# The first two modulation rows of a conditioned encoder layer: weights as the stationary operand, three feature tiles ahead

## The chip, the cores and the metric

The kernel runs on one core of a Trainium2 chip. The metric is the device time of one execution in microseconds; lower is better. Five engines work side by side, each with its own queue of instructions: TensorE (PE in the profile; its weight loads are listed apart as PEld), VectorE (DVE), ScalarE (ACT), GpSimd (POOL) and SyncE (SP), which here only issues transfers.

## The reference, cut to what matters

One layer of a streaming encoder, for a prompt of 1024 tokens and a sample of 32 tokens that share all weights (1056 tokens in all, width 1024). Each of the two groups has its own conditioning vector c.

```
mod = silu(c) @ w_ada + b_ada            # (1024) @ (1024, 9*1024): nine rows of 1024 for each group
modulate(x, k) = x * (1 + mod[3k+1]) + mod[3k]
x = layer_norm(x, ln_in_g, ln_in_b)      # shared input norm
f = swiglu(modulate(x, 0), ffn1_w1, ffn1_w3, ffn1_w2)
x = layer_norm(ALPHA * x + 0.5 * (1 + mod[2]) * f, ...)
...                                      # mixer (RG-LRU and spatial gating), then a second FFN
```

Only rows 0 and 1 of mod (shift and scale of the first FFN) are touched here. They are needed first of all: nothing of the first FFN can be multiplied before them.

## The kernel before, in words

All activations are held transposed: features on the 128 partitions, tokens along the free axis, in three chunks of 384, 384 and 288 tokens. A feature tile f is 128 of the 1024 features; there are eight. Every large matmul works on float32 split into a high and a low part of the type float32r, as three products (high*high, high*low, low*high). The helper `mm` (L152, L153 in the profile) issues all of them; `h_mm` (L565) issues the three products of one weight tile, one feature tile and one chunk.

The kernel begins with `startup` (L376). Nine row tiles of x (eight of 128 tokens, one of 32) come in by SP. In a loop over i, DVE takes the statistics of tile i (`stats`, L418, L419, L562), GpSimd makes the inverse root (L563), ACT (L428) or for tiles 5 and 8 DVE (L425) normalises tile i-1 (`norm`), TensorE transposes it (`turn`, L438), and ACT (L450) or, from tile 6 on, DVE (L448) copies tile i-2 out of PSUM (`out`). The first feature tile's modulation product is issued at i = 9 (`ada_mm`), behind the last turn. Then two of the four half tiles of weights of the first FFN tile are split (`w_split`: high part on ACT at L210, low part at L211).

`ffn_first` (L575) follows. For each feature tile f: `ada_t` turns the product's row into a column by two small transposes and makes the coefficients A and B of that tile with b_ada and the input norm's gain and bias (L589 to L594); `mod_a` applies them on ACT (L539); the next tile's product is issued (`ada_mm(f + 1)`) and its row copied out (`ada_row`, L515); `mod_b` makes xh and xl, the high and low parts (L548 or L546, L549); the weights of a tile further on are split (`ada_load`); and TensorE does step f - 1 of the first FFN tile (`mms`): 18 matmuls into six PSUM banks, two weight matrices by three chunks by three products.

In the product for the modulation, c is the stationary operand and w_ada streams. For feature tiles 0 to 3 both are plain float32 (silu(c), 128x2, stationary; 256 columns of w_ada moving, rows 0 and 1 side by side). For tiles 4 to 7 both are split: c4 holds high and low parts of silu(c) in four columns, and w_ada comes as high and low part. The result lies along a row: group on the partition, feature along the free axis.

In `startup` and `ffn_first` the instructions of DVE, ACT and GpSimd keep the order in which the code issues them, and those of TensorE do so throughout. Behind `ffn_first`, a planner orders DVE, ACT and GpSimd by its own estimate of when things are ready. There, work beside the main stream is issued by generators (`go`, `poll`) at due times counted in TensorE work: the residual's scaling, the other seven rows of mod (`ada_rest`, DVE, L714), and `combs` (L810), which forms sums and differences of blocks of xh and xl on GpSimd and later DVE (L801 to L804) for the fast product of the later FFN tiles.

Buffers: ring "wh" (eight tiles) holds split weights and, before them, the float32 modulation weights of tiles 0 to 3; ring "raw" (five) holds weights as they come; the pool `gpool` is opened behind `startup` in the space of its x tiles. [...]

## Time and profile before

| | us |
|---|---|
| median of three runs | 1881.07 |
| lowest, highest | 1878.71, 1882.26 |
| the profiled execution's own time | 1877.9 |
| its span, first to last instruction | 1876.1 |
| first transposes start | 10.74 |
| first FFN matmul starts | 40.75 |
| granted TensorE clock, mean | 0.994 |

In the timeline rows, the columns are start, duration, engine, line, operation, output and inputs, shapes (stationary, then moving for a matmul), the number of merged instructions, and in brackets how long the engine had been idle and what ended that. In rows of groups, "busy, mean ns of one" stand behind the bar, then the idle time ahead of them. Rows of windows give, for a stretch of time, its length, each engine's busy time, then the granted clock, the share of the DMA engines and GB/s. A float32 product that isn't float32r has more than one record in the trace.

### The profile page before, as it was taken

How to read it: one execution, taken by the hardware profiler on the slowest of the kernel's cores; microseconds unless marked ns; L12 is line 12 of the kernel's file. 1: busy time of each engine (PE TensorE's matmuls, PEld its weight loads, DVE VectorE, ACT ScalarE, POOL GpSimd, SP SyncE). 2: the span in 40 equal slices, each digit the busy share in tenths (PEclk: the TensorE clock that was granted, in tenths of full speed). 3: DMA queues.
4: the chain of work that ended last, by engine and by line, in shares of the span. 5: the costliest groups of instructions: out<-in, count | busy, mean ns of one | idle time of the engine just before them, and what ended most of it. 6: DMA issues, size and time to landing. Idle time of an engine off the chain costs nothing.

```text
span 1876.1 us, 28307 instructions
## 1 busy us (share of the span) xinstructions
PE 1823.0 (97%) x11295; PEld 1784.8 (95%) x11295; DVE 1329.9 (71%) x2362; ACT 684.0 (36%) x1200; POOL 556.2 (30%) x416
## 2 busy tenths in 40 slices
PE   6999999999999999999999999999999999999997
PEld 3889999999999999989889999999999999999996
DVE  6889878978888866873986476965655564555676
ACT  5551332233233223355554447132232233223324
POOL 2493434243333424022000000134233333423410
PEclk9999999999999999999999999999999999999998
DMA  7352353444445433212012300120121112011102
GB/s 295 124 181 68 124 191 124 143 161 165 159 130 189 136 115 125 90 75 88 4 53 81 136 25 33 45 68 23 46 67 46 45 46 68 26 59 52 46 1 93
DMA packets 51028, 175.70 MB, mean 94 GB/s; under 512 B 7504, under 2 KB 10192, under 8 KB 50128
## 3 DMA queue, kind: packets, MB, share of 16 engines
q1 hardware_dynamic: 31984, 102.77, 16.4%
q10 hardware_dynamic: 18912, 71.11, 11.0%
q8 instruction: 89, 1.46, 0.3%
q14 instruction: 43, 0.35, 0.1%
HBM read 165.13 MB, written 8.74 MB: 93 GB/s over the span
## 4 chain that ended last, share of the span: by engine, by line
PE 81%; DVE 10%; ACT 3%; POOL 3%; issue 1%; DMA 1%; SPq 0%; ACTq 0%; DVEq 0%; POOLq 0%
PE ps L153 79%; DVE xl L549 1%; PE psl L153 1%; DVE wh L211 1%; POOL s L801 1%; ACT t L539 1%; DVE xa L960 1%; PE psa L153 1%; POOL tx L804 1%; DVE araw L714 1%; POOL s L802 1%; POOL tx L803 0%; ACT xh L546 0%; DVE s L801 0%; POOL raw L242 0%
## 5 line engine op out<-in xcount | busy, mean ns | idle before, releaser
L153 PE MATMUL ps<-xh,wh 128*128 128x384 f32 (+1 forms) x3824 | 900.8, 318 | 2.6 <-ACT xh L546 1.8
L153 PEld LDWEIGHTS ps<-xh,wh 128*128 128x128 f32 x3824 | 660.8, 188 | 6.2 <-ACT xh L546 2.2
L153 PE MATMUL ps<-xl,wh 128*128 128x384 f32 (+1 forms) x1912 | 607.7, 318 | 4.8 <-DVE xl L549 4.7
L210 ACT ACTIVATE wh<-raw 128x512 fp32r<-128x512 f32 x452 | 281.9, 629 | 596.2 <-PE ps L153 471.2
L153 PE MATMUL ps<-g,wh 128*128 128x384 f32 (+1 forms) x2808 | 459.4, 323 | 1.9 <-DVE s L675 0.8
L153 PEld LDWEIGHTS ps<-g,wh 128*128 128x128 f32 x2808 | 453.1, 188 | 3.6 <-DVE s L675 1.1
L211 DVE TENSOR_TENSOR wh<-raw,wh 128x512 fp32r<-128x512 f32 x283 | 214.0, 760 | 229.6 <-ACT wh L210 226.9
L153 PEld LDWEIGHTS ps<-xl,wh 128*128 128x128 f32 x1912 | 359.2, 188 | 9.0 <-DVE xl L549 7.9
L211 POOL TENSOR_TENSOR wh<-raw,wh 128x512 fp32r<-128x512 f32 x169 | 246.3, 1459 | 385.6 <-ACT wh L210 384.7
L960 DVE SCALAR_TENSOR_TENSOR xb<-ps,gt,xb 128x384 f32<-128x384 f32 (+1 forms) x352 | 151.4, 484 | 77.9 <-PE ps L153 64.7
L714 DVE SCALAR_TENSOR_TENSOR araw<-araw,cb 128x1024 f32<-128x1024 f32 x112 | 160.0, 1432 | 11.8 <-DMA araw<-ada 7.8
L153 PE MATMUL ps<-tx,wh 128*128 128x384 f32 x912 | 167.1, 338 | 0.0
L240 POOL TENSOR_TENSOR raw<-raw 128x512 f32<-128x512 f32 x38 | 54.5, 1433 | 365.8 <-DVE wh L211 348.5
L153 PEld LDWEIGHTS ps<-tx,wh 128*128 128x128 f32 x912 | 159.8, 188 | 0.0
L960 DVE SCALAR_TENSOR_TENSOR xa<-ps,gt,xa 128x384 f32<-128x384 f32 (+1 forms) x320 | 135.2, 480 | 7.2 <-PE ps L153 7.0
L210 ACT ACTIVATE g<-s 128x384 fp32r<-128x384 f32 (+1 forms) x126 | 61.4, 494 | 164.4 <-DVE s L675 164.4
L852 DVE TENSOR_TENSOR s<-s,ps 128x384 f32<-128x384 f32 x152 | 83.8, 552 | 45.0 <-PE ps L153 43.2
L211 DVE TENSOR_TENSOR g<-s,g 128x384 fp32r<-128x384 f32 (+1 forms) x126 | 93.5, 748 | 21.6 <-ACT g L210 20.5
L563 POOL TENSOR_TENSOR r<-r,half 128x3 f32<-128x3 f32 x8 | 7.1, 886 | 305.7 <-DVE r L562 305.7
L153 PE MATMUL ps<-T,wh 128*128 128x384 f32 x456 | 85.6, 335 | 0.0
L242 POOL TENSOR_TENSOR raw<-raw 128x512 f32<-128x512 f32 x38 | 57.5, 1513 | 85.9 <-DVE wh L211 83.6
L153 PEld LDWEIGHTS ps<-T,wh 128*128 128x128 f32 x456 | 80.2, 188 | 0.0
(246 smaller groups left out, 1649.3 us busy)
## 6 DMA issues: line engine op xcount, KB each, us to landing
raw<-wst SPq DMA_DIRECT2D x156, 512.0 KB, 3.7
araw<-ada ACTq DMA_DIRECT2D x112, 512.0 KB, 3.4
wnat<-ada SPq DMA_DIRECT2D x8, 512.0 KB, 10.2
raw<-ada SPq DMA_DIRECT2D x8, 512.0 KB, 4.0
xt<-x SPq DMA_DIRECT2D x7, 512.0 KB, 8.0
araw<-wst ACTq DMA_DIRECT2D x6, 512.0 KB, 4.1
sp<-xa ACTq DMA_DIRECT2D x2, 1536.0 KB, 5.3
xb<-sp ACTq DMA_DIRECT2D x2, 1536.0 KB, 9.3
```

Of the source, the lines that this page charges most:

```text
L153: self.nc.tensor.matmul(out, a, b, start=start, stop=stop, skip_group_check=True)
L210: self.nc.scalar.activation(dst_h, src, AF.Copy)
L211: (e or self.nc.vector).tensor_tensor(dst_l, src, dst_h.bitcast(F32), ALU.subtract)
L240: G.tensor_tensor(a["A21"], a["A11"], a["A21"], ALU.subtract)
L242: G.tensor_tensor(a["A22"], a["A22"], a["A21"], ALU.subtract)
L539: self.nc.scalar.activation(tmp[:, j, a:a + w], X[:, k, a:a + w], AF.Identity, scale=self.A[:, s, k, v:v + 1], bias=self.B[:, s, k, v:v + 1])
L549: V.tensor_tensor(xl, tmp, xh.bitcast(F32), ALU.subtract)
L714: V.scalar_tensor_tensor(raws[n], raws[n], 1.0, cb, ALU.mult, ALU.mult, accum_out=self.mod[:, m, f, v:v + 1])
L801: e.tensor_tensor(r, x[i][:, k, :].bitcast(F32), y[i][:, k, :].bitcast(F32), op)
L802: e.tensor_tensor(t, t, u, ALU.add)
L852: self.mark = V.tensor_tensor(out, x, ps[:, :n], ALU.add)
L960: self.mark = V.scalar_tensor_tensor(X[:, m, a + o:a + o + w], ps[:, o:o + w], self.gt[:, s, m, v:v + 1], X[:, m, a + o:a + o + w], ALU.mu ...
```

## The change

The product is turned round. The weights of w_ada become the stationary operand, 128x128 in plain float32, and silu(c) moves, two columns (one for each group). The result comes out as a column, features on partitions, two numbers each, for rows 0 and 1 in four columns of one PSUM bank. So the row copy, the small transposes, the splits of c and of w_ada, and the float32r products of tiles 4 to 7 are gone; `ada_t` reads PSUM directly with three DVE operations for every tile. The host's layout of tiles 0 to 3 loses its special order.

The order changes too. Tile 0's weights are loaded between x4 and x5; tiles 1 to 3 behind the first two weight tiles of the FFN; tiles 4 to 7 at the head of `ffn_first`, into `gpool`, as they are. `ada_mm(0)`, `(1)` and `(2)` are issued in the loop of `startup` at i = 4, 7 and 9, behind turns 3, 6 and 8; `ada_t(0)` and `(1)` at i = 5 and 8. All four half tiles of the first FFN tile's weights are split in `startup`. In `ffn_first`, iteration f issues `ada_mm(f + 3)`, `mod_a(f + 1)`, `mod_b(f)`, `ada_t(f + 2)` and then step f, not step f - 1.

```diff
@@ run, startup
-        self.c4 = c.tile([P, K, 4], F32R, name="c4")
...
+            if i == 4:
+                self.ada_load(0)
+        self.w_raw()
+        self.w_raw()
+        for f in range(1, 4):
+            self.ada_load(f)
...
-        self.split(self.c4[:, :, 0:2], self.c4[:, :, 2:4], self.cs)
...
             if 0 < i < 10:
                 norm(i - 1)
                 turn(i - 1)
-            if i == 9:
-                self.ada_mm(0)
+            if i in (4, 7, 9):
+                self.ada_mm((4, 7, 9).index(i))
+            if i in (5, 8):
+                self.ada_t((5, 8).index(i))
             if i > 1:
                 out(i - 2, i > 7)
-        for h in range(2):
-            self.w_split()
+            if i >= 9:
+                self.w_split()
+                self.w_split()
         es.close()
@@ new ada_load, ada_mm, ada_t
+    def ada_load(self, f):
+        if f < 4:
+            w = [self.wpool.tile([P, K, P], F32, tag="wh", name="adw", bufs=RING) for _ in range(2)]
+        else:
+            w = self.gpool.tile([P, 2, K, P], F32, tag="ggtt"[f - 4].replace("t", "tx"), name="adx", bufs=2)
+            w = [w[:, 0], w[:, 1]]
+        for m in range(2):
+            self.nc.sync.dma_start(w[m], self.i["ada0"][2 * f + m])
+        self.ada_w.append(w)
+
     def ada_mm(self, f):
         ps = self.ps("psa")
         self.rows[f] = ps
+        for m in range(2):
             for k in range(K):
+                self.mm(ps[:, 2 * m:2 * m + 2], self.ada_w[f][m][:, k, :], self.cs[:, k, :], k == 0, k == K - 1, passes=4)
+                self.pe += 0.2
+
+    def ada_t(self, f):
+        V = self.nc.vector
...
+        mod = self.mod[:, 0:2, f, :]
+        V.tensor_tensor(mod, self.rows.pop(f)[:, 0:4].rearrange("p (m q) -> p m q", m=2),
+                        b_ada[:, 0:2, f:f + 1].to_broadcast([P, 2, 2]), ALU.add)
+        V.scalar_tensor_tensor(self.AB[:, 0, :, f, :], self.mod[:, 1:2, f, :].to_broadcast([P, 2, 2]), 1.0,
+                               gb[:, :, f:f + 1].to_broadcast([P, 2, 2]), ALU.add, ALU.mult)
+        V.tensor_tensor(self.B[:, 0, f, :], self.B[:, 0, f, :], self.mod[:, 0, f, :], ALU.add)
@@ ffn_first
-        lows = []
-        self.ada_row(0)
+        for f in range(4, K):
+            self.ada_load(f)
+        t = mod_a(0)
         for f in range(K):
-            ada_t(f, self.rows.pop(f))
-            t = mod_a(f)
-            for low in lows:
-                low()
-            lows.clear()
-            if f + 1 < K:
-                self.ada_mm(f + 1)
-                self.ada_row(f + 1)
+            if f + 3 < K:
+                self.ada_mm(f + 3)
             if f == 0:
                 w = [self.w_get((f"f{nf}w1", 0))]
-                self.w_split(nc.gpsimd)
-                self.w_split(nc.gpsimd)
                 w.append(self.w_get((f"f{nf}w3", 0)))
                 pss = [[self.ps() for _ in range(3)] for _ in range(2)]
+            if f + 1 < K:
+                t1 = mod_a(f + 1)
             mod_b(f, t)
-            for d in (False, True):
-                if self.n_ada < 16:
-                    lows.append(self.ada_load(d))
-            if f == 1:
+            t = t1
+            if f + 2 < K:
+                self.ada_t(f + 2)
+            if f == 0:
                 self.resid_coef(0, self.v("lnin_g"), self.v("lnin_b"))
-            if f >= 5:
+            if f >= 3:
                 while self.n_raw < 6:
                     self.w_raw()
             if f >= 6:
                 self.w_split(nc.gpsimd)
                 self.w_split(nc.gpsimd)
-            if f:
-                mms(f - 1)
+            if f + 1 < K:
+                mms(f)
         mms(K - 1)
```

## The prediction

> **What bounds the kernel now.** I read the page first (busy shares, chain of waits), then TensorE's timeline over the first 85 us, then what its neighbours did there.

> ```profile
> PE 1823.0 (97%) x11295; PEld 1784.8 (95%) x11295; DVE 1329.9 (71%) x2362; ACT 684.0 (36%) x1200; POOL 556.2 (30%) x416
> PE 81%; DVE 10%; ACT 3%; POOL 3%; issue 1%; DMA 1%; SPq 0%; ACTq 0%; DVEq 0%; POOLq 0%
> ```

> TensorE sets the time. The change rewrites only the stage in which it is not full: from the first transposes to the end of the first FFN tile's eight steps. What comes behind is a full TensorE, so microseconds won at that stage's end count whole, if no later wait gives them back. The stage on TensorE:

> ```profile
> 10.74 1.97 PE L438 MATMUL ps<-idn,xt 128*128 128x128 f32 x8 [10.74 <-ACT xt L428]
> ...
> 16.63 1.09 PE L438 MATMUL ps<-idn,xt 128*128 128x128 f32 x8 [0.89 <-ACT xt L428]
> ...
> 21.80 1.09 PE L438 MATMUL ps<-idn,xt 128*128 128x128 f32 x8 [1.11 <-ACT xt L428]
> 23.90 1.70 PE L438 MATMUL ps<-idn,xt 128*128 128x128 f32 x16 [1.00 <-ACT xt L428]
> 25.53 3.62 PE L153 MATMUL psa<-wnat,cs 128*2 128x256 f32 x16
> 31.01 0.25 PE L585 MATMUL psa<-idn,arow 2*128 2x2 f32 x2 [1.86 <-DVE arow L515]
> 31.19 5.30 PE L153 MATMUL psa<-wnat,cs 128*2 128x256 f32 x16
> 37.00 0.28 PE L585 MATMUL psa<-idn,arow 2*128 2x2 f32 x2 [0.51 <-DVE arow L515]
> ...
> 40.75 0.45 PE L153 MATMUL ps<-xh,wh 128*128 128x384 f32 x1
> ...
> 51.72 2.08 PE L153 MATMUL psa<-adx,c 128*4 128x128 f32 x32
> ...
> 80.68 0.51 PE L153 MATMUL ps<-xh,wh 128*128 128x384 f32 x2
> ...
> 83.10 0.47 PE L153 MATMUL ps<-xh,wh 128*128 128x288 f32 x2
> ```

> Turn 3 is the row at 16.63, turn 6 at 21.80, turns 7 and 8 at 23.90. The eight steps of 18 matmuls run from 40.75 to 83.25: the second of the pair at 83.10 opens the next FFN tile. From 80.68 (third of a step) to 83.25 are 16 matmuls, 0.161 us each, so 2.90 a step, 23.2 for eight. The other 19.3 us are modulation matmuls, their transposes, and waits.

> **Removed.** Four tiles' products of 3.62 (one 5.30) and four of 2.08, two small transposes a tile, the row copies, and eight splits (ACT, with a DVE or GpSimd half). **Added.** 16 float32 products a tile, 128x128 weights stationary, two columns moving. The trace has this operation in the layer norms, with one column:

> ```profile
> 784.03 0.72 PE L153 MATMUL psl<-ones,t 128*128 128x1 f32 x6
> ...
> 814.75 0.80 PE L153 MATMUL psl<-ones,t 128*128 128x1 f32 x6 [1.20 <-DVE t L1218]
> ...
> 783.86 0.81 PEld L153 LDWEIGHTS psl<-ones,t 128*128 128x128 f32 x6
> 814.73 0.74 PEld L153 LDWEIGHTS psl<-ones,t 128*128 128x128 f32 x6 [1.49 <-issue]
> ```

> Six records are three products there, as the 16 records at 25.53 are eight: two loads a product. After an idle TensorE, six loads of 0.19 take 0.74, so they start every 0.11, and the matmul hides behind its load. A tile is 32 records: **3.5 us**. Bounds: 0.094 a record (the six matmuls at 784.03: 0.72 less one of 0.25, over five) gives 3.0; 0.124 (the loads at 783.86, the first pulled ahead under other work) gives 4.0. I take 0.11, the stretch with nothing around it.

> [...]

> **Moved: the start-up, a chain in order.** DVE, ACT and GpSimd keep the written order here.

> ```profile
> 16.11 1.28 DVE L418 BATCH_NORM_STATS2 bs<-xt 128x6 f32<-128x512 f32 x2
> ...
> 18.46 1.28 DVE L418 BATCH_NORM_STATS2 bs<-xt 128x6 f32<-128x512 f32 x2
> ...
> 22.50 1.29 DVE L448 COPY xa<-ps 128x512 f32<-128x512 f32 x2 [0.61 <-PE ps L438]
> 23.70 0.79 DVE L425 TENSOR_SCALAR xt<-xt,mv,rs 32x1024 f32<-32x1024 f32 x1
> ...
> 31.30 0.17 DVE L589 TENSOR_TENSOR mod<-psa,vec 128x4 f32<-128x4 f32 x1 [0.44 <-PE psa L585]
> ...
> 31.69 0.16 DVE L594 TENSOR_TENSOR AB<-AB,mod 128x2 f32<-128x2 f32 x1
> ```

> Tile 0's products follow turn 3: 17.6 to 21.1. Its coefficients (ada_t, three DVE operations, 0.5 by 31.30 to 31.69) stand in DVE's queue behind the statistics of x5, which were done by 16.1 (18.7 with the later x5 below); DVE now sits until the products land, 21.25. Queued behind: statistics of x6 and the normalising of x5, so turn 5, and through them all later turns. DVE goes on at 21.75; x6's statistics and x5's norm take 2.35 (16.11 to 18.46): 24.1. From there to turn 6 before took 3.34 (18.46 to 21.80): 27.45, and the turn 0.95: 28.4. Tile 1's products run to 31.9, DVE waits for them again (to 32.05), its coefficients 0.5, copying turn 6 out 1.2 (22.50 to 23.70): 33.75. From x8's norm to the end of turn 8 took 1.83 (23.70 to 25.53): 35.6. Then tiles 2 and 3 back to back: **42.6**, the first FFN matmul, 1.85 later than before. Meanwhile DVE copies turns 7 and 8 and makes the low halves of w1 and w3, all four now here (0.7 each), and the first xh, xl: about 41.5, 1 us to spare.

> Loop: tiles 4 to 7 and eight steps: 14 + 23.2, and 0.1 at each of some four changes between them: end at **80.1**, against 83.25. DVE and ACT are one to two steps ahead here (0.44 and 0.87 us an operation, six a step, under the 6.4 us of a step; rows next), and lose the adx splits; so I cost the scaling and splitting at nothing. Without that cover it would be 3.9 us a step on the path.

> ```profile
> L549 DVE TENSOR_TENSOR xl<-t,xh 128x384 fp32r<-128x384 f32 (+1 forms) x21 | 18.2, 868 | 3.3 <-ACT xh L546 2.6
> L548 DVE CAST xh<-t 128x384 fp32r<-128x384 f32 (+1 forms) x20 | 8.8, 441 | 0.5 <-ACT t L539 0.5
> ```

> **Transfers.** Tile 0's 1 MB now goes ahead of x5 to x8 on SP.

> ```profile
> 20.00:30.00 10.00, 7.04 (x47) 4.02 (x45) 6.34 (x16) 5.11 (x8) 1.08 (x2) 1.00 1.03 409
> ...
> DMA to landing us min/median/max: 9.3/10.2/10.4
> ...
> 7.62 4.31 SPq L399 DMA_DIRECT2D wnat<-ada  x4
> ...
> raw<-ada SPq DMA_DIRECT2D x8, 512.0 KB, 4.0
> ```

> At 409 GB/s (the last column) a MB is 2.6 us. The first ada tile landed by 17.8 behind 1.7 MB of x that it now precedes: 15, in time for 17.6. x5 to x8 land 2.6 later; DVE, held until 21.75, does not notice. Tiles 4 to 7 lie where the start-up's x lay, and SP waits for that, at worst until turn 8 at 35.6. Then 1 MB each and 4.0 to land: tile 4 by 42.2 (wanted at 42.6 + 2.9 = 45.5), tile 7 by 50 (wanted at 64.7). Queued behind them are only the second FFN tile's weights, wanted after 70. Costed at nothing; what covers it is the 3.3 us of slack of tile 4.

> **The clock.** TensorE has new holes: 22.0 to 24.2 and 25.1 to 27.4, around turn 5.

> ```profile
> 29.00:30.00 1.00, 0.15 (x1) 0.00 (x0) 0.15 (x1) 0.63 (x1) 0.00 (x0) 1.00 1.02 401
> 31.00:32.00 1.00, 0.99 (x6) 0.52 (x7) 0.49 (x3) 0.05 (x1) 0.00 (x0) 0.94 0.98 344
> 32.00:33.00 1.00, 1.00 (x3) 0.26 (x2) 0.00 (x0) 1.00 (x2) 0.00 (x0) 0.50 0.95 352
> ```

> After one hole of 1.9 us the granted clock halved for some 3.4 us (that is the 5.30). Two such holes in 5.4 us make one drop likely, over turn 6 and tile 1. Cold transposes took 1.97 for eight against 1.09 warm, 1.8 times; 3.2 us of cold work lose 1.4. Between 0 and 2.8 (two drops), I take **1.4**: end at 81.5. [...]

> **What is late next.** Behind the stage TensorE has one large wait, for the third FFN tile's g:

> ```profile
> PE ps L153 <- DVE gt L211: 7.5, 1, 7.5
> ...
> 82.09 5.39 DVE L211 TENSOR_TENSOR wh<-raw,wh 128x512 fp32r<-128x512 f32 x4 [0.92 <-ACT wh L210]
> ...
> 138.66 0.56 DVE L801 TENSOR_TENSOR s<-tx,xh 128x384 f32<-128x384 f32 x1 [1.60 <-POOL s L802]
> ```

> DVE waits 1.60 in it for GpSimd's combinations. In the new loop tile 7's products end at 80.1 - 4 x 2.9 = 68.5; coefficients, scaling (0.5 + 2.1) and the last xh, xl (3.9) end near 75, five us ahead of TensorE, where they ended with it; DVE's four low halves (5.39 under GpSimd's traffic) start earlier, and GpSimd's chain gains on TensorE. I take the 1.6 back, and 0.5 of the slower operations there: **-2.1**. Bounds: -7.5 (the whole wait goes), +2 (the planner orders DVE anew from there on, and the wait grows as much as one or two DVE operations of that row's kind).

> **Sum.** -3.15 (80.1 against 83.25), +1.4, -2.1: **-3.9 us**. The span goes from 1876.1 to 1872.2, the profiled execution from 1877.9 to 1874.0; the median of the runs shown lies 3.2 above that execution, so **1877.2** on its scale. 0.2%, what a measurement can tell from nothing here, is 3.8 us: the forecast lies on that edge.

> **Rivals.**
> Weights at half rate (slower): the loop is 3.5 us of loads, then 2.9 of streaming; if one or two moving columns don't count as work for the clock, it halves from tile 2 on. No long run of such products is in the trace to exclude it; against it speaks that the transposes, also half loading, kept full clock from 16 to 26. It decides from 122 ns a record (eight tiles lie on the path; 52.1 + 8 x 3.89 = 83.25). At 1.8 times 0.11 the tiles cost 6.3: the stage ends 8 x 2.8 later than forecast, +19 against before, about 1900. Chance 0.15.
> The start-up eats it (no change): the clock's loss as taken, and the wait at 137 us stays 7.5 because DVE's order there moves: -1.75, 1879.3. For it: DVE is serial there. Chance 0.27, 0.04 of it slower (4.0 a tile, a second drop and the planner's +2 together make +5.7).
> More is won: 3.0 a tile (-7.1), +1.4, and half of the 7.5: -9.5, 1871.6. Chance 0.10.
> Three tiles ahead isn't reached: tile 4 comes late to its buffer. The slack of 3.3 must go first; with twice the wait, 4 us are lost, and the time is the old one, 1881. Chance 0.03.
> The forecast has 0.45, 0.34 of it beyond the edge.

> **Numbers.** Faster 0.34 + 0.10 = 0.44; same 0.11 + 0.23 + 0.03 = 0.37; slower 0.15 + 0.04 = 0.19. Bounds together: -7.1 + 0 - 7.5 is not likely at once; the best of the loads and half the wait give 1870, the worst (4.0 a tile, so +0.9 for the stage, +2.8, 0) 1884.8. The half-rate case is left out: 1870 to 1885.

> **What would show it.** Two-column products every 0.11 us at full clock; DVE held near 21 and 32 us before ada_t; the first FFN matmul at 42.6 to 44; the next FFN tile at 80 to 81.5; the wait near 135 us at 5 to 6. Wrong if a tile takes over 3.9, if DVE is not held, or if the time moves behind 150 us.

## The result, and the profile after

| us | before | after |
|---|---|---|
| median of four runs of each, beside each other | 1881.66 | 1899.53 |
| lowest, highest | 1878.71, 1882.94 | 1897.03, 1905.23 |
| the profiled execution's own time | 1877.9 | 1900.79 |
| its span | 1876.1 | 1899.1 |
| first FFN matmul starts | 40.75 | 54.12 |
| second FFN tile starts (the stage's end) | 83.25 | 104.5 |
| granted TensorE clock, mean | 0.994 | 0.978 |

The changed kernel takes 1.0109 times the time of the kernel before (95% interval 1.0093 to 1.0125; the ratio of the two medians alone is 1.0095): 18 us longer by the medians, where 4 us less were forecast. Of the 23.0 us between the two spans, 21.3 lie ahead of the second FFN tile.

From the page of the changed kernel, its busy shares, the row of the granted clock in 40 slices of 47.5 us, and the chain; in the second fence the clock's row of the kernel before:

```profile
PE 1851.0 (97%) x11343; PEld 1825.8 (96%) x11343; DVE 1309.0 (69%) x2347; ACT 676.4 (36%) x1191; POOL 540.3 (28%) x410
...
PEclk7698999999999999999999999999999999999999
...
PE 86%; DVE 6%; POOL 3%; ACT 2%; DMA 2%; issue 1%; SPq 0%; ACTq 0%; POOLq 0%; DVEq 0%
```
```profile
PEclk9999999999999999999999999999999999999998
```

TensorE is as full as before; it is slower. The clock's row was all nines before but for the last slice; here its first slices, in which the stage of the change lies, stand at 7, 6 and 9. (The 8 in the fourth, 142 to 190 us, belongs to a wait behind the stage; it is taken up further below.) TensorE's timeline of that stage, after:

```profile
17.98 4.30 PE L153 MATMUL psa<-cs,adw 128*128 128x2 f32 x32
22.14 1.95 PE L426 MATMUL ps<-idn,xt 128*128 128x128 f32 x8
25.37 1.94 PE L426 MATMUL ps<-idn,xt 128*128 128x128 f32 x8 [1.28 <-DVE xt L413]
...
30.01 6.83 PE L153 MATMUL psa<-cs,adw 128*128 128x2 f32 x32
...
40.44 13.81 PE L153 MATMUL psa<-cs,adw 128*128 128x2 f32 x64
54.12 0.67 PE L153 MATMUL ps<-xh,wh 128*128 128x384 f32 x1
...
59.00 4.34 PE L153 MATMUL psa<-cs,adx 128*128 128x2 f32 x32
...
68.59 3.76 PE L153 MATMUL psa<-cs,adx 128*128 128x2 f32 x32
...
76.61 4.85 PE L153 MATMUL psa<-cs,adx 128*128 128x2 f32 x32
...
86.24 4.29 PE L153 MATMUL psa<-cs,adx 128*128 128x2 f32 x32
```

A tile's 32 records take 3.76 us at best, 6.83 at worst. Taking one matmul's tail off a row (0.25 off the 3.76, 0.4 off the 13.81), a record starts every 0.113 or 0.213 us: the first, the forecast's 0.11, at a granted clock of 1.00 (69 to 71 us), the second at 0.50 (41 to 54 us). Tiles 2 and 3, back to back, run at half rate throughout (13.81). The clock itself, in one-microsecond windows of the same kernel (behind the engines' busy times stand the granted clock, the share of the DMA engines and GB/s):

```profile
20.00:21.00 1.00, 1.00 (x10) 1.00 (x9) 0.00 (x0) 0.07 (x1) 0.00 (x0) 0.87 1.06 422
21.00:22.00 1.00, 1.00 (x7) 1.00 (x7) 0.00 (x0) 0.00 (x0) 0.00 (x0) 0.50 1.02 406
```
```profile
58.00:59.00 1.00, 1.00 (x8) 1.00 (x6) 0.00 (x0) 0.00 (x0) 0.00 (x0) 0.85 0.00 0
61.00:62.00 1.00, 1.00 (x10) 1.00 (x9) 0.00 (x0) 0.00 (x0) 0.00 (x0) 0.85 0.00 0
68.00:69.00 1.00, 1.00 (x9) 1.00 (x7) 0.00 (x0) 0.00 (x0) 0.00 (x0) 0.73 0.00 0
71.00:72.00 1.00, 1.00 (x11) 1.00 (x11) 0.00 (x0) 0.00 (x0) 0.00 (x0) 0.97 0.00 0
75.00:76.00 1.00, 1.00 (x6) 1.00 (x6) 0.38 (x1) 0.14 (x1) 0.00 (x0) 0.82 0.00 0
78.00:79.00 1.00, 1.00 (x11) 1.00 (x10) 0.00 (x0) 0.00 (x0) 0.00 (x0) 0.89 0.00 0
85.00:86.00 1.00, 1.00 (x6) 1.00 (x6) 0.00 (x0) 0.00 (x0) 0.00 (x0) 0.70 0.00 0
89.00:90.00 1.00, 1.00 (x7) 1.00 (x6) 0.00 (x0) 0.00 (x0) 0.00 (x0) 0.51 0.00 0
95.00:96.00 1.00, 1.00 (x5) 1.00 (x5) 1.00 (x2) 1.00 (x4) 1.00 (x2) 0.58 0.00 0
```

The mean of a window in which the clock switches once between 1 and 0.5 gives the moment. It fell at 20.74, rose at 58.30, fell at 61.70, rose at 68.54, fell at 71.94, rose at 75.36, fell at 78.78, rose at 85.60, fell at 89.02, rose at 95.84. From one to the next it is 3.40 to 3.42 us, or two or eleven times that (6.82 to 6.84, 37.56). What fills the 3.41 us ahead of each goes with it in this trace: ahead of every fall mostly the products of a tile (17.98, 59.00, 68.59, 76.61, 86.24), ahead of every rise the matmuls of a step (54.12, then those behind each tile). Stretches that hold some of both (61.70 to 65.11, 78.78 to 82.19) leave it at 0.50. TensorE and its weight loads are busy for the whole of each window shown, and in those from 58 us on the DMA engines move nothing (the last column), so neither idleness nor other traffic slows the products there. The first fall comes ahead of the hole of 1.28 us (22.14 + 1.95 = 24.1 to 25.37), with tile 0's products still running.

### The profile page after: what moved, and what is told of

The parts are those of the page before. It is cut to its first block, busy times and chain, and to the rows that moved or that the text cites. A ratio compares the mean times of both kernels' runs of the same rounds, so it can differ in the third digit from the quotient of the medians.

```text
span 1899.1 us, 28354 instructions
## 1 busy us (share of the span) xinstructions
PE 1851.0 (97%) x11343; PEld 1825.8 (96%) x11343; DVE 1309.0 (69%) x2347; ACT 676.4 (36%) x1191; POOL 540.3 (28%) x410
## 4 chain that ended last, share of the span: by engine, by line
PE 86%; DVE 6%; POOL 3%; ACT 2%; DMA 2%; issue 1%; SPq 0%; ACTq 0%; POOLq 0%; DVEq 0%
PE ps L153 82%; PE psa L153 2%; PE psl L153 1%; POOL s L750 1%; ACT t L511 1%; POOL s L751 1%; POOL tx L753 1%; DMA xt<-x 1%; DMA adw<-ada 1%; DVE wh L211 1%; DMA araw<-ada 0%; PE psz L153 0%; ACT xh L518 0%; DVE araw L663 0%; POOL tx L752 0%
## 5 line engine op out<-in xcount | busy, mean ns | idle before, releaser
L153 PE MATMUL ps<-xh,wh 128*128 128x384 f32 (+1 forms) x3824 | 907.0, 320 | 0.4 <-ACT s L808 0.3
L153 PEld LDWEIGHTS ps<-xh,wh 128*128 128x128 f32 x3824 | 667.1, 190 | 2.7 <-ACT s L808 1.2
L153 PE MATMUL ps<-xl,wh 128*128 128x384 f32 (+1 forms) x1912 | 610.9, 320 | 2.9 <-DVE xl L521 2.8
L210 ACT ACTIVATE wh<-raw 128x512 fp32r<-128x512 f32 x452 | 281.8, 628 | 602.9 <-PE ps L153 492.4
L153 PE MATMUL ps<-g,wh 128*128 128x384 f32 (+1 forms) x2808 | 463.0, 325 | 3.2 <-ACT g L210 2.5
L153 PEld LDWEIGHTS ps<-g,wh 128*128 128x128 f32 x2808 | 456.7, 189 | 4.9 <-ACT g L210 2.8
L211 DVE TENSOR_TENSOR wh<-raw,wh 128x512 fp32r<-128x512 f32 x285 | 212.3, 749 | 230.1 <-ACT wh L210 226.7
L153 PEld LDWEIGHTS ps<-xl,wh 128*128 128x128 f32 x1912 | 362.5, 190 | 5.7 <-DVE xl L521 4.6
L211 POOL TENSOR_TENSOR wh<-raw,wh 128x512 fp32r<-128x512 f32 x167 | 241.8, 1449 | 426.4 <-ACT wh L210 425.8
L153 PE MATMUL ps<-tx,wh 128*128 128x384 f32 x912 | 164.3, 336 | 0.0
L663 DVE SCALAR_TENSOR_TENSOR araw<-araw,cb 128x1024 f32<-128x1024 f32 x112 | 155.4, 1391 | 12.3 <-DMA araw<-ada 7.7
L153 PEld LDWEIGHTS ps<-tx,wh 128*128 128x128 f32 x912 | 157.2, 188 | 0.0
L210 ACT ACTIVATE g<-s 128x384 fp32r<-128x384 f32 (+1 forms) x126 | 61.3, 493 | 159.6 <-DVE s L624 154.9
L801 DVE TENSOR_TENSOR s<-s,ps 128x384 f32<-128x384 f32 x152 | 83.9, 552 | 45.7 <-PE ps L153 44.2
L211 DVE TENSOR_TENSOR g<-s,g 128x384 fp32r<-128x384 f32 (+1 forms) x126 | 93.6, 748 | 21.0 <-ACT g L210 20.1
L153 PE MATMUL ps<-T,wh 128*128 128x384 f32 x456 | 85.7, 336 | 0.0
L153 PEld LDWEIGHTS ps<-T,wh 128*128 128x128 f32 x456 | 80.1, 188 | 0.0
## 6 DMA issues: line engine op xcount, KB each, us to landing
raw<-wst SPq DMA_DIRECT2D x156, 512.0 KB, 3.7
araw<-ada ACTq DMA_DIRECT2D x112, 512.0 KB, 3.5
adw<-ada SPq DMA_DIRECT2D x8, 512.0 KB, 10.0
adx<-ada SPq DMA_DIRECT2D x8, 512.0 KB, 11.6
xt<-x SPq DMA_DIRECT2D x7, 512.0 KB, 8.2
araw<-wst ACTq DMA_DIRECT2D x6, 512.0 KB, 4.3
```

The costliest lines, as they stand in the source:

```text
L153: self.nc.tensor.matmul(out, a, b, start=start, stop=stop, skip_group_check=True)
L210: self.nc.scalar.activation(dst_h, src, AF.Copy)
L211: (e or self.nc.vector).tensor_tensor(dst_l, src, dst_h.bitcast(F32), ALU.subtract)
L663: V.scalar_tensor_tensor(raws[n], raws[n], 1.0, cb, ALU.mult, ALU.mult, accum_out=self.mod[:, m, f, v:v + 1])
L801: self.mark = V.tensor_tensor(out, x, ps[:, :n], ALU.add)
```

## The experiments

**First set: is it the two columns?** Theory: the clock goes by the columns that are moved through the array, and a stretch with little but weight loads counts as idle. Rivals: the holes around turn 5 set the clock back and the order of the start-up keeps it there; or the loads simply take longer than 0.11 us beside other traffic. The first kernel moves the same two columns 32 times over, read with stride 0; `ada_t` reads the first two of them, and everything else is as after. The second moves them 8 times over (16 columns).

```diff
-                self.mm(ps[:, 2 * m:2 * m + 2], self.ada_w[f][m][:, k, :], self.cs[:, k, :], k == 0, ...)
+                cw = self.cs[:, k, :].unsqueeze(1).to_broadcast([P, 32, 2])
+                self.mm(ps[:, 64 * m:64 * m + 64], self.ada_w[f][m][:, k, :], cw, k == 0, ...)
```

(Where the expectations count columns against a load's time, they count one of plain float32 twice. That is an estimate from the kernel before: its 16 records of 256 columns at 25.53 take 3.62, 0.88 ns a column, and the float32r matmuls behind 80.68, 0.161 us for some 350 columns, 0.46 ns. By it 128 moving columns last as long as a load, 0.113 us, and the transposes from 16 to 26 us, 40 of 128 columns and eight of 32, counted once, a quarter of the time.)

> The kernel after, but each modulation product moves 64 columns (the same two, read 32 times over) where it moved two; the weights loaded, their number and the order of everything stay. Theory A (the clock counts columns that stream through the array; weight loads count for nothing): 128 columns stream in the time of each 128-column load, the granted clock stays at 1.0 from 20 to 95 us, a load record stays at 0.11 us, the stage ends near 80 to 82 us instead of 104, and the time is 1877 to 1880. Theory B (holes of TensorE in the start-up drop the clock, and the number of columns is of no matter): clock 0.5 from 21 to 58 us as in the kernel after, time near 1899. Theory C (plain float32 products with 128x128 weights are slow as such): records of 0.21 and the time near 1899, too.

> As before with 16 columns, 32 streamed in each load of 128. Theory A with a threshold as low as the transposes (which kept full clock from 16 to 26 us in the kernel before with a quarter of the time streaming or less): clock 1.0, 1877 to 1880. Theory A with a threshold near a third to a half: clock falls as in the kernel after, 1890 to 1900. Theories B and C: 1899.

The third puts 48 such products into the kernel before, behind the eighth step, where TensorE has no hole.

```diff
         mms(K - 1)
+        ps = self.ps("psd")
+        for j in range(48):
+            self.mm(ps[:, 0:2], self.xacc[0][:, j % 8, 0:P], self.cs[:, j % 8, :], j == 0, j == 47)
```

> The kernel before with 48 products more, float32, 128x128 weights stationary (x, as it lies), two columns moving, into a PSUM bank that nobody reads; they stand behind the eighth step of the first FFN tile, where TensorE has no hole ahead of or behind them. At 0.11 us a record (96 records) they cost 10.5 us. Theory A: the clock halves within 3.4 to 6.8 us of their start, the rest takes 0.21 a record, and up to 3.4 us of the matmuls behind run at half rate: 15 to 19 us slower than before, with a stretch at 0.5 in the profile. Theory B (holes): no drop, 10 to 11 us slower.

The fourth keeps the turned product with two columns and takes the order of before: tile 0's product at i = 9, one tile ahead in the loop, no DVE operation held in the start-up.

```diff
-            if i in (4, 7, 9):
-                self.ada_mm((4, 7, 9).index(i))
-            if i in (5, 8):
-                self.ada_t((5, 8).index(i))
+            if i == 9:
+                self.ada_mm(0)
...
-            if f + 3 < K:
-                self.ada_mm(f + 3)
+            self.ada_t(f)
+            t = mod_a(f)
+            if f + 1 < K:
+                self.ada_mm(f + 1)
...
-            if f + 1 < K:
-                mms(f)
+            if f:
+                mms(f - 1)
```

> The turned product alone: the kernel after with tile 0's product behind the last turn and tiles 1 to 7 one ahead in the loop, as the kernel before had them (the loads stay as in the kernel after). Theory A: each tile's 32 two-column records between steps lower the clock as they did at 59 to 95 us in the kernel after; tiles of 3.5 to 6.8 us, some steps at half rate; stage end 90 to 100 us, 1887 to 1898. Theory B: fewer holes in the start-up than in the kernel after, so clock 1.0 in the loop and a stage end near 80, 1876 to 1882.

Measured: 64 columns 1890.08 (1.0057, 1.0037 to 1.0076), 16 columns 1898.37 (1.0101, 1.0073 to 1.0129), the run of 48 in the kernel before 1889.76 (1.0055, 1.0037 to 1.0074), the old order 1899.93 (1.0101, 1.0071 to 1.0130); the kernel before 1879.59 beside them.

With 64 columns half of the loss is back, not all of it as Theory A expected, and the timeline (first fence) and the windows (second) split it cleanly:

```profile
24.17 1.06 PE L426 MATMUL ps<-idn,xt 128*128 128x128 f32 x8 [2.21 <-DVE xt L413]
...
28.80 6.93 PE L153 MATMUL psa<-cs,adw 128*128 128x64 f32 x32
...
39.34 13.91 PE L153 MATMUL psa<-cs,adw 128*128 128x64 f32 x64
...
57.34 3.68 PE L153 MATMUL psa<-cs,adx 128*128 128x64 f32 x32
```
```profile
25.00:26.00 1.00, 0.23 (x3) 0.00 (x0) 0.93 (x5) 0.25 (x1) 0.28 (x1) 0.65 1.02 406
...
40.00:45.00 5.00, 5.00 (x26) 5.00 (x25) 4.57 (x12) 2.40 (x5) 0.00 (x0) 0.50 0.94 338
...
60.00:65.00 5.00, 5.00 (x40) 5.00 (x38) 2.83 (x9) 2.11 (x4) 0.00 (x0) 1.00 0.00 0
```

In the loop, with the same loads, the clock now stays at 1.00 (60 to 65 us) and a tile takes 3.68. But it fell at 25.3 us, behind the hole of 2.21 ahead of turn 5, and the long run of tiles 1 to 3 at 64 columns (6.93 and 13.91 us) did not raise it again: 0.50 up to the first step. So the holes do cost something here, and in this run 64 columns held a full clock and did not bring one back. With 16 columns the products are as slow as with two: tiles 4 to 7 take 17.2 us together in both, at a mean clock of 0.976 and 0.978 over the span.

The run of 48 shows the fall with no hole near it, in the kernel before: the timeline's row, and windows.

```profile
83.42 17.57 PE L153 MATMUL psd<-cs,xa 128*128 128x2 f32 x96
```
```profile
84.00:86.00 2.00, 2.00 (x20) 2.00 (x20) 2.00 (x2) 0.63 (x2) 2.00 (x3) 1.00 0.32 61
86.00:88.00 2.00, 2.00 (x14) 2.00 (x14) 2.00 (x3) 0.00 (x0) 1.08 (x1) 0.65 1.02 393
...
90.00:92.00 2.00, 2.00 (x11) 2.00 (x11) 2.00 (x3) 0.56 (x2) 2.00 (x2) 0.50 0.45 180
```

A window of 2 us holds 20 records ahead of the fall at 86.6 and 11 behind it, with TensorE and its loads at 2.00 of 2.00 in each. The time alone would not have told this: 10 us more is what the holes' theory gave. The trace tells it, for a later wait shrank by about as much as the low clock cost (rows in the second set).

At two columns the old order costs as much as the new one, with tiles 0 to 2 in one run of 20.64 us. That run by itself doesn't exclude the holes: its clock fell at 23.6 us, behind a hole of 1.72 and ahead of tile 0. In the loop its five tiles take 3.73 to 4.88 us, where two columns take 3.63 at full clock (third set) and 6.83 at half (the changed kernel's tile 1); and the third set has a kernel without holes.

**Second set: with wide products, what is the rest of the change worth?** 128 columns, as many as the load brings in, in the changed kernel; the same with `ada_t(0)` and `(1)` moved back behind the loop's later turns, so that DVE is not held for them; that at 64 columns; and the run of 48 at 128 columns, to weigh the clock by itself. The widths are edited as above; the move is

```diff
-            if i in (5, 8):
-                self.ada_t((5, 8).index(i))
+            if i == 8:
+                self.ada_t(0)
             if i > 1:
                 out(i - 2, i > 7)
+            if i == 10:
+                self.ada_t(1)
```

> The kernel after with 128 moving columns a product (the two read 64 times over): 256 columns stream in each load's time, a full stream. In w64 the clock held in the loop (1.0 from 57 us) but, once down at 25 us in the holes round turn 5, it stayed down until the first FFN matmuls. Theory A with a higher bar for rising than for staying: now tile 1's products raise the clock within 3.4 to 6.8 us of 28 us, tiles 2 and 3 run at 0.11 to 0.12 a record (3.5 to 3.8 a tile), the stage ends at 81 to 84 instead of 92, 1878 to 1884. If the low clock from 25 to 55 us has nothing to do with columns: stage end near 92 and 1890 as in w64.

> w128, with ada_t of tile 0 at i = 8 and of tile 1 at i = 10, behind the copies out, so DVE is no longer held for tile 0's and 1's products and the holes of TensorE at 22 to 24 and 25 to 27 us go. Theory: no drop of the clock at all; turns 7 and 8 end near 31, first FFN matmul near 38, stage end near 75 to 77, 6 to 8 us earlier than in the kernel before; behind the stage I allow 5 us of loss, as the kernel after and w64 had between their stage and the first layer norm: 1873 to 1880. If the drop is not made by the holes, it is there again at 25 us and nothing is won against w128.

> The same with 64 columns. Theory A with two bars: the clock, never dropped, holds at a half stream; stage end as in w128_free, or up to 2 us earlier if 128 columns stretch a record beyond its load; 1872 to 1880. If a half stream does not hold it in a long run of products (tiles 2 and 3 are 7 us without a pause), it falls there at 34 to 38 us and the time is near 1885.

> run_of_48 with 128 moving columns. There the run took 17.6 us and the time rose by 10.2, as a later wait fell from 7.5 to 1.6. Theory A: the run takes 10.5 to 11.5 us at clock 1.0, no matmul behind it is slowed; the later wait shrinks less, for the other engines have 7 us less to catch up in; 3 to 8 us slower than before. If columns are of no matter: 17.6 us again and 10 slower.

Measured, beside 1880.09 for the kernel before: 128 columns 1880.28 (1.0000, 0.9988 to 1.0011); with DVE free 1870.79 (0.9956, 0.9939 to 0.9973); that at 64 columns 1870.78 (0.9957, 0.9943 to 0.9971); the wide run of 48 1883.38 (1.0015, 1.0001 to 1.0029).

At 128 columns, the timeline of the changed kernel:

```profile
27.84 1.97 PE L426 MATMUL ps<-idn,xt 128*128 128x128 f32 x8 [1.81 <-ACT xt L416]
29.60 5.51 PE L153 MATMUL psa<-cs,adw 128*128 128x128 f32 x32
...
38.33 7.41 PE L153 MATMUL psa<-cs,adw 128*128 128x128 f32 x64
```

Here the clock falls in the hole too (the cold turn 6 at 27.84), but it comes back within tile 1 (5.51, between 3.74 and 6.9): it stands at 0.50 from 26.5 to 33.3 us. The loop from 45.50 on takes 37.6 us, as forecast, and the stage ends at 83.1. With DVE not held, no fall is left; the windows have one row for the whole stage:

```profile
24.86 3.74 PE L153 MATMUL psa<-cs,adw 128*128 128x128 f32 x32
...
30.02 7.41 PE L153 MATMUL psa<-cs,adw 128*128 128x128 f32 x64
```
```profile
15.00:75.00 60.00, 58.00 (x455) 57.33 (x454) 40.38 (x104) 33.23 (x59) 10.96 (x10) 1.00 0.58 224
```

The first FFN matmul starts 3.6 us sooner than in the kernel before, the second FFN tile at 74.8 instead of 83.25. This version and its twin at 64 columns are 9 us faster than the kernel before.

The wide run of 48 takes 11.19 us where the narrow one took 17.57:

```profile
83.54 11.19 PE L153 MATMUL psd<-cs,xa 128*128 128x128 f32 x96
```

The difference, 6.4 us, is that of the two medians (1889.76 and 1883.38, against 1879.59 and 1880.09 beside them). So what the low clock takes from the run comes out at the end, as nearly as medians with intervals of some 3 us to each side can tell; the two profiled spans (1886.4 and 1881.8) are 4.6 apart. The wide run also shows 11.2 us of pure TensorE work that cost 3.3: the waits of TensorE in the stretch of the third tile's g give most of the rest. They are these, in the kernel with the narrow run and in the one with the wide run; in the kernel before they are 7.5 and 0.8:

```profile
PE ps L153 <- DVE gt L211: 1.6, 1, 1.6
```
```profile
PE ps L153 <- DVE s L679: 2.1, 1, 2.1
```

**Third set: the two parts and the bound.** Two columns with DVE free, 32 columns with DVE free, and the turned product alone at 128 columns in the order of before. They are made of the edits shown. (In the second expectation, the 27 and 108 are nanoseconds of one load; at 128 columns 32 records take 3.49 us, 109 each.)

> The kernel after, two columns, with DVE not held (ada_t of tile 0 at i = 8, of tile 1 at i = 10): the holes round turn 5 go, which were enough to drop the clock in w64 and w128. If narrow products lower it by themselves, tile 0's 3.5 us do it (as they did at 20.7 us in the kernel after), and nearly nothing is won: 1893 to 1900. If the holes were needed for the fall, the clock holds and the time is that of w128_free, 1871.

> w64_free with 32 columns: half a load's time (64 of 128 columns) is not streamed in twice over, 27 us of stream in 108 of loads. 64 columns held the clock there, 16 did not in w16. If the bar for staying lies at a quarter of the time or below, as the transposes before tile 0 suggest (a quarter, and full clock): clock 1.0, 1871. If it lies between a quarter and a half: it falls in tiles 2 and 3, 1880 to 1895.

> old_order with 128 columns: the turned product alone with the clock kept up. Each tile in the loop costs 3.6 where it cost 3.62 + 0.28 (tiles 1 to 3) or 2.08 + 0.28 (4 to 7), and no splits; but one tile ahead leaves the chain product, coefficients, scaling, splitting of DVE and ACT (0.5 + 2.1 + 2.4 and more) beside 2.9 us of matmuls. I expect a stage end of 80 to 84 and 1876 to 1881: about nothing against before. If the clock is the whole of what made old_order slow, this is the run that shows it, 18 to 22 us below it.

Measured, beside 1879.72: two columns with DVE free 1892.61 (1.0075, 1.0057 to 1.0093); 32 columns 1883.59 (1.0020, 1.0002 to 1.0037); the product alone, wide, 1877.91 (0.9997, 0.9984 to 1.0009).

```profile
16.97 3.63 PE L153 MATMUL psa<-cs,adw 128*128 128x2 f32 x32
...
31.60 13.81 PE L153 MATMUL psa<-cs,adw 128*128 128x2 f32 x64
```
```profile
21.00:22.00 1.00, 1.00 (x9) 1.00 (x8) 1.00 (x2) 0.87 (x2) 0.48 (x1) 0.72 1.03 410
```
```profile
31.47 9.82 PE L153 MATMUL psa<-cs,adw 128*128 128x32 f32 x64
...
46.38 3.94 PE L153 MATMUL psa<-cs,adx 128*128 128x32 f32 x32
...
54.41 3.65 PE L153 MATMUL psa<-cs,adx 128*128 128x32 f32 x32
```
```profile
22.00:23.00 1.00, 1.00 (x9) 1.00 (x8) 1.00 (x4) 0.41 (x1) 0.55 (x1) 0.64 1.02 406
```

The first two fences are two columns. From tile 0 on TensorE idles 0.2 us in the whole start-up, and yet the clock falls at 21.4 us, behind 3.41 us that are mostly tile 0, and tiles 2 and 3 are as slow as in the changed kernel (13.81): it falls here without a hole. The other two are 32 columns. The clock fell behind tile 0 (22.3 us), rose again, and fell in the run of tiles 2 and 3 (9.82, between 7.4 and 13.8). In the loop, where steps lie between, it fell once more, over tile 4 (3.94), and stayed full over tiles 5 to 7. Two columns and 128, both in the old order, are 22 us apart (1899.93 and 1877.91), and the wide one is level with the kernel before: turning the product round is by itself worth nothing that these runs can tell.

All stages side by side, from the profiled executions (us; the two kernels with the run of 48 left out). The last two columns are the time from the second FFN tile to the end of the span, and how many times 3.41 us the clock stood at half in it, by the clock record of the trace, without the last stretch that runs into the end:

| columns, order | first FFN matmul | second FFN tile | span | ratio to before | behind the stage | 3.41 us at half |
|---|---|---|---|---|---|---|
| before | 40.75 | 83.25 | 1876.1 | 1 | 1792.9 | 3 |
| 2, changed | 54.12 | 104.5 | 1899.1 | 1.0109 | 1794.5 | 4 |
| 2, old order | 47.75 | 104.4 | 1899.4 | 1.0101 | 1795.0 | 5 |
| 2, DVE free | 45.28 | 95.4 | 1890.3 | 1.0075 | 1794.9 | 5 |
| 16, changed | 52.69 | 102.8 | 1901.1 | 1.0101 | 1798.3 | 7 |
| 32, DVE free | 41.10 | 82.6 | 1881.0 | 1.0020 | 1798.4 | 6 |
| 64, changed | 53.02 | 92.0 | 1886.8 | 1.0057 | 1794.9 | 4 |
| 128, changed | 45.50 | 83.1 | 1878.2 | 1.0000 | 1795.1 | 4 |
| 128, old order | 37.34 | 79.3 | 1875.5 | 0.9997 | 1796.2 | 5 |
| 64, DVE free | 36.87 | 74.5 | 1873.0 | 0.9957 | 1798.5 | 6 |
| 128, DVE free | 37.19 | 74.8 | 1868.4 | 0.9956 | 1793.6 | 3 |

The part behind the stage differs by up to 5.6 us from one execution to another, though the edits all lie ahead of it. By an estimate, half of 3.41, each of those at half clock costs up to 1.7 us; less 1.7 for each, the column runs from 1786.4 to 1788.5. So differences of a few microseconds between two single spans here are mostly those of the clock, and it takes the medians, or the stage's end, to tell the versions apart.

## Why the prediction was wrong, and where it was right

**The step that failed** is the clock: "Between 0 and 2.8 (two drops), I take 1.4". It priced the holes and nothing else. Against the rival of half-rate weights it said that "the transposes, also half loading, kept full clock from 16 to 26". That row was misread: a transpose moves 128 columns over its 128x128 weights, the added product moves two. Transposes are the row for the kernel with 128 columns, whose clock did behave like theirs (1.00 from 45 to 83 us). The rows that the forecast had of narrow products, the layer norms' six records in 0.7 us, are far shorter than the 3.41 us that lie between the clock's changes. So the trace of before did not decide the question, and a chance of 0.15 rested on an argument from a row that did not bear on it. What the runs show in its place: with two columns the clock went to half behind tile 0 with no hole ahead of it (21.4 us with DVE free), and 22 us lie between two and 128 columns in one and the same order.

**The rival that came true** was half-rate weights, with +19 and about 1900; 1899.53 was measured. The clock did halve with two columns moving, though from tile 0 on and not from tile 2 (the first fall is at 20.74); its sum holds only by luck. It put 2.8 us on each of eight tiles, and left the steps alone. In the trace tiles 0 to 3 take 24.9 (4.30 + 6.83 + 13.81), and tiles 4 to 7, which it had at 6.3 each, 17.2 together, 3.2 more than the forecast's 14. But the loop as a whole takes 50.4 (54.12 to 104.5) instead of 37.5, so some 9.7 us were lost in the steps: behind each fall in the loop the clock stood at 0.50 for 3.4 or 6.8 us, over the matmuls of the step behind the tile (61.70 to 68.54, 71.94 to 75.36, 78.78 to 85.60, and from 89.02 to 95.84), and the first step ran at 0.50 up to 58.30.

**Right: the load's price.** 0.11 us a record and 3.5 us a tile. At 128 columns, at full clock, a tile in the loop starts at 48.47 and the next step's first matmul at 51.96, 3.49 later. The trace has two loads a product here as well, 32 records a tile. The forecast's loop of 37.5 us took 37.6 in that kernel.

**Right: DVE held.** It was forecast until 21.25 and 32.05. The coefficients' first operation, after:

```profile
22.32 0.16 DVE L484 TENSOR_TENSOR mod<-psa,vec 128x4 f32<-128x4 f32 x1 [4.85 <-PE psa L153]
...
36.87 0.16 DVE L484 TENSOR_TENSOR mod<-psa,vec 128x4 f32<-128x4 f32 x1 [8.30 <-PE psa L153]
```

The brackets are DVE's idle time for tile 0 and tile 1, later than forecast because the products are slow. What this holding costs, together with the fall of the clock that its holes bring, the kernels with 128 columns tell: 83.1 against 74.8 at the stage's end.

**Right in kind, low in size: the holes.** One drop was forecast, with 1.4 us. At 128 columns there was one, but it lasted twice 3.41 us (26.5 to 33.3 us, 6.8) where the forecast had one of 3.4; it added 0.9 to turn 6 (1.97 against 1.1) and 1.8 to tile 1 (5.51 against 3.74): 2.7, at the upper bound. With it the first FFN matmul comes at 45.50 rather than at 42.6 to 44.

**Right: transfers, scaling and splitting at nothing.** The profile after has no wait of TensorE in the loop for them, and none for the tiles in `gpool`; nor has the kernel with 128 columns, at full clock (TensorE busy for 38.00 of 38.00 us from 45 to 83).

**Wrong: -2.1 behind the stage.** With stage end and span side by side, the changed kernel loses another 1.7 there (23.0 less 21.3), that with 128 columns 2.3 (its span is 2.1 longer although its stage ends 0.2 sooner). "GpSimd's chain gains on TensorE" came true only in part. GpSimd after:

```profile
93.92 5.88 POOL L211 TENSOR_TENSOR wh<-raw,wh 128x512 fp32r<-128x512 f32 x4 [64.80 <-ACT wh L210]
99.76 1.47 POOL L750 TENSOR_TENSOR s<-xh,xh 128x384 f32<-128x384 f32 x1
...
108.59 1.02 POOL L750 TENSOR_TENSOR s<-xh,xh 128x384 f32<-128x384 f32 x1 [5.96 <-DVE g L211]
```

It starts its combinations 4.7 us ahead of the stage's end (before, at 84.06, 0.8 behind it), and then stands 5.96 us for the low half of g, which DVE makes from the stage's sums. TensorE's waits for the third tile's g fall from 8.3 (7.5 and 0.8) to 7.1, the first line here:

```profile
PE ps L153 <- DVE gt L211: 7.1, 2, 5.8
...
PE ps L153 <- ACT g L210: 2.5, 1, 2.5
```

That is 1.2 won of the 2.1. Two things that the sum doesn't have took it back. The second line is another wait for a g, 273 us behind the stage's end, and it was 0.6 before. And the clock fell in the wait for the third tile's g, before (first row) and after:

```profile
141.00:148.00 7.00, 3.21 (x12) 3.21 (x13) 7.00 (x11) 0.44 (x1) 2.69 (x2) 0.51 0.43 151
160.00:171.00 11.00, 6.52 (x21) 6.09 (x22) 10.01 (x20) 0.61 (x2) 1.86 (x2) 0.53 0.55 191
```

It stood at half for 6.8 us before (141.1 to 147.9) and for 10.2 after (160.7 to 170.9), by the same estimate up to 1.7 us of matmuls more. With 128 columns, too, it is 3.41 us more than before (the table's last column).

So with the clock repaired and all else as in the change, the sum would have been -3.15 + 3.0 + 2.3, about +2 in that one execution, and 1.0000 in the medians: the rival "the start-up eats it".

**Open.** Why some executions lose some of the clock behind the stage where others don't (from 784 to 1184 us its mean is 0.99 with 128 columns in the changed order, 1.00 with DVE free) was not taken apart, nor the 2 us that are left there. How many columns keep the clock up was not narrowed below the steps 32, 64 and 128, and 32 columns among steps, which lost the clock over one tile of four, were tried in one kernel only.

## What to carry to other kernels

A product with few moving columns and a fresh weight load for each looked like full work in the busy shares here, at a granted clock of 0.50: read the granted clock in windows of a few microseconds ahead of trusting "97% busy". Where such products run for microseconds (here 3.5 a tile), try moving the columns several times over: at 128 for a 128x128 load that cost 0.1 us a tile here (3.74 against 3.63) and gave back 19 to 22 us, at 64 with DVE free as much as at 128 (1870.78 and 1870.79). And don't let an engine that works in order wait for a result that is wanted later: with the clock repaired, moving the few small DVE operations of two tiles made the difference between no gain and 9 us.
